# A transformer block on one Trainium2 core: the first half of the values taken from x before it is normalised, the second half moved up behind it

## The chip, the cores and the metric

The kernel runs on one core of a Trainium2 chip. The core has five engines with an instruction stream each: TensorE (matmuls; PE in the profile, its weight loads PEld), VectorE (DVE), ScalarE (ACT), GpSimd (POOL) and SyncE (SP, which only issues DMAs). The metric is the device time of one execution in microseconds; a profiled execution has its own time, and a span from its first to its last instruction.

## The reference, cut to what is computed

One layer, one batch row, 1024 tokens, width 1024, 16 heads of 64, all in fp32:

```python
mod = c_act @ ada_w[l] + ada_b[l]            # c_act = silu(c)
sh1, sc1, g1, sh2, sc2, g2 = [m[:, None, :] for m in jnp.split(mod, 6, axis=-1)]
h = rmsnorm(x, ln1_g[l]) * (1.0 + sc1) + sh1
p = h @ w_in[l]
q, k, v, cb, cc, cx, ga, gb = jnp.split(p, split_at, axis=-1)
q = rmsnorm(q.reshape(b, s_len, SB_HEADS, SB_HEAD_DIM), q_norm_g[l])
k = rmsnorm(k.reshape(b, s_len, SB_HEADS, SB_HEAD_DIM), k_norm_g[l])
y_a = stick_breaking_attention(q, k, v)
y_b = cb * causal_dwconv(cc * cx, conv_w[l])
merged = (jax.nn.sigmoid(ga) * (y_a @ w_branch_a[l])
          + jax.nn.sigmoid(gb) * (y_b @ w_branch_b[l]))
x = x + g1 * (merged @ w_out[l])
h = rmsnorm(x, ln2_g[l]) * (1.0 + sc2) + sh2
f = (jax.nn.silu(h @ w_ffn_gate[l]) * (h @ w_ffn_up[l])) @ w_ffn_down[l]
x = x + g2 * f
```

The attention has no softmax. For a block of 128 queries and the keys up to it, the weight of key s is sigmoid(z_ts) times the product of 1 - sigmoid(z_tj) over the keys j between s and t. The kernel gets that product from a scan along the keys, and multiplies the scanned values with the differences of neighbouring rows of v, plus the last row of v of each block.

The value projection is linear, which the change uses: with a = ln1_g (1 + sc1), row t of v is (1/rms_t) times (x_t a) @ W, plus sh1 @ W, and the last term is one row, the same for every token.

## The kernel before, in words

Every fp32 product is made of three fp32r matmuls. An operand is split into a high part (ScalarE, an activation that rounds) and a low part (VectorE, operand minus high part); the product is high x high, high x low, low x high, summed in one PSUM bank. PSUM has eight banks of 128 x 512. Each matmul goes over 128 rows of the contraction, so a product over the width of 1024 has 8 steps of three matmuls.

The stages, with their places in the profile (us from the start of the span):

- **Opening, 0 to 72.** x is loaded twice: by tokens (`xq`), for the mean square of each token, and transposed (`xts`, by channels). L184 loads `cab`, the row c broadcast to 128 partitions. Silu(c) is made of it with a Sigmoid and a product. For each tile of 128 channels, `mod_sum` (L246 to L254) makes two dot products of 1024 columns on VectorE (L250), one for the scale and one for the shift; `norm_x` (L287) multiplies the tile with a and 1/rms, where `bcast` (L277 to L279) has spread 1/rms over the partitions with fp32 matmuls; `make_hi` (L292, ScalarE) and `make_lo` (L296, VectorE) add the shift and split. `mm_tok` (L299 to L309) multiplies 128 tokens with the weights. In the opening it takes the first 512 columns of the values: 8 token tiles x 8 channel tiles x 3 matmuls, all eight PSUM banks open at once. Eight fp32 matmuls over raw tokens (L262) stand ahead. `finish_v` (L417 to L423) copies the result and stores it to `d_v[0]`. The loads come in order on SyncE's queue.
- **Key projection, 72 to 134.** `mm_tok` again, two times 8 tiles of 512 columns. `finish_k` normalises them by heads and turns them. Beside it, the generator `factors()`, driven by `more()`, builds on VectorE the sums of tiles of x that later products use (`xts`, `ts`, `dsh` of L137 and L371) and writes them to DRAM.
- **Gates, queries and the convolution's inputs, to 566**, by products of sums of blocks (L132 to L134, combined on VectorE at L137).
- **Attention, 566 to about 997.** Per head and block i of 128 queries: `att_scores` (L808, L809: z, then a Sigmoid on ScalarE at L810), `att_scan` (L818, VectorE, length 128 (i + 1)), `att_trans` (L832 transposes on TensorE, L835 high part on ScalarE, L836 low part on VectorE) and, for every second block, `att_av` (L847, L848). The transposes of block i - 2 and the products of block i - 3 come with the scores of block i (`attention`, L863 on). `att_dv` makes the differences of the value rows (vb minus va, L137) and splits them; `load_v` and `load_vlast` read the values back.
- **Fillers.** Between the steps of attention, TensorE takes other matmuls from the generator `fillers()` (L912 on): first the second half of the values (L927 to L929, 256 columns at a time, two groups of 256, 16 tiles), then the gated convolution (16 tiles, L908 to L910 with evacuation L137), then the projection of branch B (16 tiles, L908 to L910), whose evacuation multiplies with the sigmoid of gate B (L982, VectorE) and goes to `d_mb`. The first 16 yields of it (HEAD) come ahead of the heads. What is left then is spread by a count: each step of attention yields a number (F_Z per bank of scores, F_T per transposed block), each filler step yields 1.3 or 0.65, and `fill` (L994) keeps the two sums in the proportion `ratio`. So these numbers, and not the time that things take, set the order on TensorE.
- **Branch A, 997 to 1100.** Its projection, times the sigmoid of gate A, plus `mb` of branch B. Then the output projection, the second norm and the FFN to the end.

The order on TensorE, and that of attention's instructions on VectorE, is the order of the program text and of the counts above.

Of the kernel before, what the change touches and what calls it, by code (L numbers as in the profile page):

```python
# [9 lines left out]
F32 = mybir.dt.float32  # L10
# [20 lines left out]
def block_kernel(tc, x, x_t, cols, ada_1, ada_2, ada_row, w_q, w_kv, w_v1, w_cg, w_a, w_b, w_o, w_g, w_u, w_d, out):  # L31
# [38 lines left out]
    d_v = [drp.tile([n, P + 1, KT, P], F32, name=f"d_v{n}_{e}") for e, n in enumerate((4, 2, 2))]  # L70
# [5 lines left out]
    d_mb = drp.tile([KT, P, T], F32, name="d_mb")  # L76
    d_g = [drp.tile([P, D], F32, name=f"d_g{e}") for e in range(2)]
# [15 lines left out]
    nc.scalar.activation(one, one, AF.Sigmoid)  # L93
# [75 lines left out]
    sa_ = ExitStack()  # L169
    adp = sa_.enter_context(tc.tile_pool(name="adp", bufs=1, side="right", reuse_waits="tile"))  # L170
# [9 lines left out]
    xqs = [bigp.tile([P, 4, D], F32, tag="big", bufs=4, name=nm("xq")) for n in range(2)]  # L180
    xq = [xqs[i // 4][:, i % 4, :] for i in range(8)]
    rs = sp.tile([P, T], F32, name="rs")
    cab = sp.tile([P, D], F32, name="cab")
    nc.scalar.dma_start(cab, ada_row[0:1, :].broadcast_to([P, D]))  # L184
    hh = [big() for n in range(2)]
    junk = [h_[:, :2, :].rearrange("p a t -> p (a t)") for h_ in hh]

    def load_xq(i0_, i1_):
        for i in range(i0_, i1_):
            nc.sync.dma_start(xq[i], x[i * P:(i + 1) * P, :])  # L190
# [3 lines left out]

    wq = []
    MC0, MC = 3, 2
    ads = []

    def load_ada(e):
        ad = adp.tile([P, 2, D], F32, tag="ada", bufs=2, name=nm("ada")) if e % 3 < 2 else sp.tile(  # L200
            [P, 2, D], F32, tag="ada", bufs=1, name=nm("ada"))
        nc.sync.dma_start(ad, ada_1[e])
        ads.append(ad)
# [26 lines left out]

    load_xq(0, 4)
    load_ada(0)
    load_xq(4, 8)
    load_x(0)
    load_wq(0)
    load_ada(1)
    load_x(1)
    load_ada(2)
    load_x(2)
    load_wq(1)  # L240
    load_x(3)
# [4 lines left out]
    def mod_sum(e):  # L246

        msum = sp.tile([P, 2], F32, tag="msum", bufs=2, name=nm("msum"))
        for m in range(2):
            nc.vector.tensor_tensor_reduce(out=ads[e][:, m], in0=ads[e][:, m], in1=cab, scale=1.0, scalar=0.0, op0=ALU.mult,  # L250
                                           op1=ALU.add, accum_out=msum[:, m:m + 1])
        nc.vector.scalar_tensor_tensor(out=a1[:, e:e + 1], in0=msum[:, 1:2], scalar=acp[:, e:e + 1],
                                       in1=ln1[:, e:e + 1], op0=ALU.add, op1=ALU.mult)
        nc.scalar.activation(mod[:, 0, e:e + 1], msum[:, 0:1], AF.Identity, bias=acol[:, 0, e:e + 1])  # L254


    ss1 = sp.tile([P, 8], F32, name="ss1")
    rsp = [ps_tr() for n in range(2)]
    warm = ps_pj()
    rts = []  # L260
    for i in range(8):
        nc.tensor.matmul(warm, ident, xq[i][:, :512], start=True, stop=True)  # L262
        if i % 2:
            nc.vector.tensor_tensor_reduce(out=junk[1], in0=xq[i], in1=xq[i], scale=1.0, scalar=0.0, op0=ALU.mult,
                                           op1=ALU.add, accum_out=ss1[:, i:i + 1])
        else:
            nc.scalar.activation(junk[0], xq[i], AF.Square, accum_out=ss1[:, i:i + 1])
        if i == 1:
            nc.scalar.activation(rs, cab, AF.Sigmoid)
            nc.vector.tensor_tensor(out=cab, in0=cab, in1=rs, op=ALU.mult)  # L270
        if i % 4 == 3:
            rts.append(rstd_of(ss1[:, i - 3:i + 1], 1.0 / D, sp, 4, eng=nc.vector))
        if i == 3:
            mod_sum(0)
            load_ada(3)
# [60 lines left out]
    for k in range(KT - 1):  # L336
# [11 lines left out]
        if k % 2 == 0:  # L348
            load_wq(k // 2 + 2)
# [1279 lines left out]
```

## Time and profile before

| | |
|---|---|
| time, median of 3 executions | 1825.74 us (1823.97 to 1827.85) |
| the profiled execution | 1827.39 us, its span 1825.6 us |
| TensorE's granted clock, mean of the span | 0.997 |
| VectorE busy | 1356.8 us, 74% of the span, 1957 instructions |
| ScalarE busy | 794.9 us, 44%, 1494 instructions |
| GpSimd busy | 368.5 us, 20%, 277 instructions |
| HBM read, written | 245.22 MB, 110.66 MB |

Read it like this. Busy time is summed per engine over the whole span; TensorE's share is quoted with the prediction. A row of the groups has the line, the engine, the operation, what it writes and reads, the tile, a count, the busy time with the mean of one instruction in ns, and the idle time of that engine just ahead with what ended most of it. A row of a timeline has the start, the duration (of one, or with x8 of a run of eight records), the engine, the line and the operation, and in brackets the wait ahead of it with its releaser. A row of the windows has the stretch A:B, its length, the busy time with the count of instructions for TensorE, its weight loads, VectorE, ScalarE and GpSimd, then the mean granted clock, the share of the DMA engines and GB/s. A row of the waits has who waited for what, with the sum in us, the count and the longest. An fp32 matmul is two records in the profile, an fp32r one is one.

### The profile page before, as it was taken

The page shows a single profiled execution, that of the slowest core. Times are in us where ns is not written, and L with a number is a line of the kernel's source. Part 1 is how long each engine was busy: PE and PEld are TensorE (multiplying, and loading weights), DVE is VectorE, ACT ScalarE, POOL GpSimd, SP SyncE. Part 2 cuts the span into 40 slices and gives each one's busy share as a digit, 9 for nine tenths or more (in the row PEclk, how much of TensorE's full clock was granted, in tenths as well). Part 3 has the DMA queues.
Part 4 walks back from the last instruction along what each step waited for, and adds up shares of the span by engine and source line. Part 5 has one row for each costly group of instructions (what it writes and reads, how often), then busy time and mean ns, then how long its engine had stood idle before and what let it go on. Part 6 is the DMA issues. An engine that isn't in the chain of part 4 may idle for free.

```text
span 1825.6 us, 24915 instructions
## 1 busy us (share of the span) xinstructions
PE 1799.5 (99%) x8829; PEld 1502.2 (82%) x8829; DVE 1356.8 (74%) x1957; ACT 794.9 (44%) x1494; POOL 368.5 (20%) x277
## 2 busy tenths in 40 slices
PE   7999999999999999999999999999999999999999
PEld 5788778887879988888888788877888888878887
DVE  7873877779872899999887554689977888644776
ACT  3452653333343666666665221663444344322321
POOL 0043328323230000000000000115534544200000
PEclk9999999999999999999999999999999999999999
DMA  9687551227748566689654546324533344299766
GB/s 394 199 319 292 181 184 69 87 84 252 273 152 247 149 180 190 196 222 304 163 141 151 174 162 217 124 88 161 196 149 140 148 166 159 104 363 325 279 230 220
DMA packets 163508, 357.50 MB, mean 196 GB/s; under 512 B 15464, under 2 KB 60848, under 8 KB 161208
## 3 DMA queue, kind: packets, MB, share of 16 engines
q1 hardware_dynamic: 130920, 289.65, 47.5%
q10 hardware_dynamic: 31456, 62.59, 9.5%
q0 software_dynamic: 1008, 3.67, 0.5%
q8 instruction: 71, 1.16, 0.3%
q14 instruction: 53, 0.43, 0.1%
HBM read 245.22 MB, written 110.66 MB: 195 GB/s over the span
## 4 chain that ended last, share of the span: by engine, by line
PE 86%; DVE 7%; DMA 4%; issue 1%; ACT 1%; POOL 0%; SPq 0%; ACTq 0%; DVEq 0%; POOLq 0%
PE e L133 7%; PE e L132 7%; PE e L134 7%; PE pj L134 5%; PE pj L132 5%; PE pj L133 5%; PE pj L309 5%; PE pj L908 5%; PE pj L910 4%; PE pj L909 4%; PE e L1456 4%; PE e L1458 4%; PE e L1457 4%; PE tr L832 3%; PE o L848 2%; PE z L808 2%
## 5 line engine op out<-in xcount | busy, mean ns | idle before, releaser
L818 DVE TENSOR_TENSOR_SCAN pt<-pt,mk 128x128 f32<-128x128 f32 (+7 forms) x128 | 172.4, 1347 | 13.0 <-ACT pt L810 13.0
L132 PE MATMUL e<-big,whi 128*128 128x512 f32 x352 | 137.9, 392 | 2.0 <-DVE c L137 2.0
L133 PE MATMUL e<-big,whi 128*128 128x512 f32 x352 | 137.7, 391 | 0.0
L134 PE MATMUL e<-big,wlo 128*128 128x512 f32 x352 | 137.5, 391 | 0.0
L123 POOL TENSOR_SCALAR rs_m<-ss 128x1 f32<-128x1 f32 x8 | 2.3, 282 | 642.9 <-ACT xn L1259 642.9
L137 DVE TENSOR_TENSOR c<-e,c 128x512 f32<-128x512 f32 x138 | 92.8, 686 | 51.4 <-PE e L134 50.5
L132 PE MATMUL pj<-big,whi 128*128 128x512 f32 x320 | 125.2, 391 | 1.4 <-DVE c L137 1.4
L134 PE MATMUL pj<-big,wlo 128*128 128x512 f32 x320 | 124.8, 390 | 0.0
L133 PE MATMUL pj<-big,whi 128*128 128x512 f32 x320 | 124.6, 389 | 0.0
L1456 PE MATMUL e<-whi,f 128*128 128x512 f32 (+1 forms) x319 | 121.8, 382 | 1.1 <-DMA f<-d_f 1.1
L137 DVE TENSOR_TENSOR c<-pj,c 128x512 f32<-128x512 f32 x140 | 93.0, 681 | 38.9 <-PE pj L134 38.4
L1457 PE MATMUL e<-wlo,f 128*128 128x512 f32 (+1 forms) x319 | 121.8, 382 | 0.0
L1458 PE MATMUL e<-whi,f 128*128 128x512 f32 (+1 forms) x319 | 121.6, 382 | 0.0
L836 DVE TENSOR_TENSOR atl<-tr,ath 128x512 fp32r<-128x512 f32 (+1 forms) x192 | 103.9, 550 | 19.4 <-ACT ath L835 17.9
L810 ACT ACTIVATE pt<-z,rq 128x512 f32<-128x512 f32 (+1 forms) x192 | 104.7, 575 | 26.6 <-PE z L809 26.4
L908 PE MATMUL pj<-big,whi 128*128 128x512 f32 x256 | 114.0, 445 | 0.0
L309 PE MATMUL pj<-whi,big 128*128 128x512 f32 x352 | 109.3, 396 | 3.9 <-ACT big L292 3.9
L137 POOL TENSOR_TENSOR ws<-raw,raw 128x512 f32<-128x512 f32 x40 | 56.3, 1407 | 275.5 <-DMA raw<-w_cg 165.8
L137 DVE TENSOR_TENSOR wlo<-raw,whi 128x512 fp32r<-128x512 f32 x116 | 88.3, 766 | 31.6 <-ACT whi L463 31.0
L463 ACT ACTIVATE whi<-raw 128x512 fp32r<-128x512 f32 x116 | 72.4, 628 | 86.9 <-PE pj L133 45.4
L835 ACT ACTIVATE ath<-tr 128x512 fp32r<-128x512 f32 (+1 forms) x192 | 93.3, 487 | 30.0 <-PE tr L832 29.1
L133 PE MATMUL e<-rl,whi 128*128 128x512 f32 x264 | 102.8, 389 | 1.5 <-DVE rl L137 1.5
(258 smaller groups left out, 4998.6 us busy)
## 6 DMA issues: line engine op xcount, KB each, us to landing
f<-d_f SPq DMA_DIRECT2D x77, 512.0 KB, 4.3
d_f<-fs SPq DMA_DIRECT2D x70, 512.0 KB, 3.2
raw<-w_cg SPq DMA_DIRECT2D x40, 512.0 KB, 3.8
raw<-w_u SPq DMA_DIRECT2D x26, 512.0 KB, 3.2
raw<-w_g SPq DMA_DIRECT2D x25, 512.0 KB, 3.4
ad<-ada ACTq DMA_DIRECT2D x19, 512.0 KB, 4.5
ada<-ada SPq DMA_DIRECT2D x8, 1024.0 KB, 11.6
d_t<-ts SPq DMA_DIRECT2D x16, 512.0 KB, 3.7
```

The source lines that it names most:

```text
L132: nc.tensor.matmul(ps, wh[:, k, :], fh[:, k, :], start=(k == 0), stop=False)
L133: nc.tensor.matmul(ps, wh[:, k, :], fl[:, k, :], start=False, stop=False)
L134: nc.tensor.matmul(ps, wl[:, k, :], fh[:, k, :], start=False, stop=(k == 3))
L137: eng.tensor_tensor(out=out, in0=a, in1=b, op=op)
L309: nc.tensor.matmul(ps, a, b, start=(k == 0 and q == 0), stop=(k == KT - 1 and q == 2))
L810: nc.scalar.activation(pt[:, off + s0:off + s0 + m], z[:, :m], AF.Sigmoid, scale=rq[:, 1, i, h:h + 1])
L818: nc.vector.tensor_tensor_scan(out=pt[:, rev], data0=pt[:, rev], data1=mk[:, rev], initial=1.0, op0=ALU.mult, op1=ALU.max)
L836: nc.vector.tensor_tensor(out=tl[:, :nb, c0:c0 + P], in0=src, in1=th[:, :nb, c0:c0 + P].bitcast(F32), op=ALU.subtract)
L908: nc.tensor.matmul(ps, wh, rh_, start=(k == 0), stop=False)
L1456: nc.tensor.matmul(o, sh, w[0][:, c], start=(j == 0), stop=False)
L1457: nc.tensor.matmul(o, sh, w[1][:, c], start=False, stop=False)
L1458: nc.tensor.matmul(o, sl, w[0][:, c], start=False, stop=(j == NJ - 1))
```

## The change

- **The opening's first half.** The first 512 columns of the values are now made from x times a, not normalised: `raw_hi` and `raw_lo` split x a1, `real` multiplies. So a step needs the scale's dot product only (`scale_sum`); the shift's comes later (`shift_sum`). The tokens' mean squares (`square`, all on ScalarE) are needed only when a result is evacuated: `finish_raw` multiplies its rows by 1/rms. Six token tiles run through all channels; the two others (`tail`) run behind, around `bcast`.
- **The shift's part** of those columns, the row sh1 @ W, is made in the key projection: `shift_row` adds up eight products of weights and shifts on VectorE into `zb`, and `put_row` sums its partitions with two small matmuls and stores the row (`d_b`) and its negative (the row that stands ahead of the first token). `turn_vlast` adds it to the last rows.
- **Silu(c)** is spread by two one-row fp32 matmuls with an activation Silu behind each, from `crow`, a load of one row in place of the broadcast one. Four fp32 matmuls on a constant (`NW = 4`) stand where the eight on tokens stood. The activation that the program starts with (its table with it) is Silu in place of Sigmoid.
- **The second half of the values** (512 columns) comes right behind, from normalised x, in the form that the opening had. The values' fillers are gone, and with them the input `w_v1`; `w_kv` has one block more.
- **Loads** of the opening: tokens and modulation share a ring of five tiles of 512 KB (`load_ring`), the modulation's two parts are loaded one by one, the tokens after the channels.
- **Gate B.** Branch B's result is copied by ScalarE to `d_mb`; the product with gate B is made in branch A on GpSimd, with the gate loaded there.
- **The counts.** F_S adds 0.05 (i + 1) or so to a block's yield, FILL is 2.0 x 16 x 5.2 in place of 2.5, HEAD counts 16 yields of 0.65. The gated convolution takes its tiles in pairs of channels.

The diff, cut:

```diff
-d_v = [... for e, n in enumerate((4, 2, 2))]
+d_v = [... for e, n in enumerate((4, 4))]
-nc.scalar.activation(one, one, AF.Sigmoid)
+nc.scalar.activation(one, one, AF.Silu)
-nc.scalar.dma_start(cab, ada_row[0:1, :].broadcast_to([P, D]))
+crow = sp.tile([1, D], F32, name="crow")
+nc.scalar.dma_start(crow, ada_row[0:1, :])
...
+def raw_hi(k):
+    for n in range(2):
+        nc.scalar.activation(hh[n][:, k, :], xt(k, n), AF.Copy, scale=a1[:, k:k + 1])
+def raw_lo(k):
+    for n in range(2):
+        nc.vector.scalar_tensor_tensor(out=hl[n][:, k, :], in0=xt(k, n), scalar=a1[:, k:k + 1],
+                                       in1=hh[n][:, k, :].bitcast(F32), op0=ALU.mult, op1=ALU.subtract)
...
+for e in range(2):
+    t = ps_pj()
+    nc.tensor.matmul(t, mk[0:1, D - P:], crow[:, e * 512:e * 512 + 512], start=True, stop=True)
+    nc.scalar.activation(cab[:, e * 512:e * 512 + 512], t, AF.Silu)
+for e in range(NW):
+    nc.tensor.matmul(warm, ident, mk[:, 512:], start=True, stop=True)
...
+for k in range(KT):
+    real(psr, k, range(MC), wq)
+    if k + 1 < KT:
+        raw_hi(k + 1)
+        split_lo(k + 1)
+    if k + 2 < KT:
+        scale_sum(k + 2)
+        split_hi(k + 2)
+    if k + 1 < KT:
+        raw_lo(k + 1)
+    real(psr, k, range(MC, NR), wq)
...
+tail(0, KB)
+for i in range(NR):
+    finish_raw(i)
...
+bcast(0)
+bcast(1)
+tail(KB, KT)
...
+            if cc == 1 and 0 < i < 6:
+                if i < 5:
+                    shift_row(i - 1)
+                else:
+                    put_row()
...
-    F_Z, F_T, F_O = 0.2,0.3,0
+    F_Z, F_T, F_S = 0.2, 0.3, 0.05
-        yield F_Z
+        yield F_Z + F_S * ((i - 1) % 8 + 1)
...
-            nc.vector.tensor_tensor(out=mb, in0=ps, in1=sb, op=ALU.mult)
+            nc.scalar.activation(mb, ps, AF.Copy)
-    FILL = 2.5 * 16 * 5.2
+    FILL = 2.0 * 16 * 5.2
-    FILL -= 1.3 * HEAD
+    FILL -= 0.65 * HEAD
...
+        sb = fp.tile([P, 512], F32, tag="yr", bufs=2, name=nm("sgb"))
+        nc.sync.dma_start(sb, d_sgb[m, :, n * 512:(n + 1) * 512])
+        nc.gpsimd.tensor_tensor(out=mb, in0=mb, in1=sb, op=ALU.mult)
```

How the order on the engines moves is shown at three places. The first is TensorE at the start of the program. Before (big is x's parts, whi and wlo the weights', dm the identity):

```order
L262 MATMUL pj_182<-xq_143,dm 128x512 x4
L262 MATMUL pj_182<-xq_144,dm 128x512 x4
L279 MATMUL tr_180<-dm,rs_r_194 128x128 x4
L279 MATMUL tr_181<-dm,rs_r_213 128x128 x4
L309 MATMUL pj_247<-whi_163,big_148 128x512
```

And now, in the lines of the changed program (mk is the constant mask):

```order
L326 MATMUL pj_173<-crow,mk 128x512
L326 MATMUL pj_176<-crow,mk 128x512
L329 MATMUL tr_172<-mk,dm 128x512 x4
L294 MATMUL pj_196<-whi_157,big_144 128x512
L294 MATMUL pj_197<-whi_157,big_144 128x512
L294 MATMUL pj_196<-wlo_158,big_144 128x512
```

The tokens' matmuls and the spread of 1/rms no longer stand ahead of the projection; the two one-row matmuls and the four on a constant do.

The second place is TensorE at the start of attention (z is a bank of scores, sqt, skh and skl are queries and keys). Before, around the first score:

```order
L808 MATMUL z_5117<-skh_4864,sqt_4863 128x128
L927 MATMUL pj_4979<-whi_4892,big_148 128x256
L928 MATMUL pj_4979<-wlo_4893,big_148 128x256
L929 MATMUL pj_4979<-whi_4892,big_217 128x256
L927 MATMUL pj_4979<-whi_4892,big_148 128x256
L928 MATMUL pj_4979<-wlo_4893,big_148 128x256
L809 MATMUL z_5117<-skl_4865,sqt_4863 128x128
L929 MATMUL pj_4979<-whi_4892,big_217 128x256
L927 MATMUL pj_5006<-whi_4878,big_149 128x256
```

And now:

```order
L900 MATMUL z_5313<-skh_5232,sqt_5231 128x128
L901 MATMUL z_5313<-skl_5233,sqt_5231 128x128
L1000 MATMUL pj_5319<-big_145,whi_5200 128x512
L1001 MATMUL pj_5319<-big_147,whi_5200 128x512
L1002 MATMUL pj_5319<-big_145,wlo_5201 128x512
L900 MATMUL z_5325<-skh_5232,sqt_5231 128x256
L901 MATMUL z_5325<-skl_5233,sqt_5231 128x256
L900 MATMUL z_5333<-skh_5232,sqt_5231 128x384
L901 MATMUL z_5333<-skl_5233,sqt_5231 128x384
...
L924 MATMUL tr_5342<-dm,pt_5193 128x128
```

The tiles of values that followed the first score are gone; the scores of the next blocks follow it with one group of three filler matmuls between, and the transpose of the first block (L924) has one more group ahead of it.

The third place is VectorE where the key projection begins (vs is a stored value tile, wlo a low part of weights, xts and dsh belong to `factors()`). Before:

```order
L420 COPY vs_582<-pj_252 128x512
L420 COPY vs_594<-tr_254 128x512
L137 TENSOR_TENSOR dsh<-mod 128x4
L63 TENSOR_TENSOR wlo_1007<-raw_1004,whi_1006 128x1024
L371 SCALAR_TENSOR_TENSOR xts<-xts,dsh 128x512 x4
L137 TENSOR_TENSOR xts<-xts 128x512 x2
```

And now:

```order
L477 COPY vs_879<-pj_576 128x512
L540 TENSOR_SCALAR zb_915<-raw_954,mod 128x512
L542 SCALAR_TENSOR_TENSOR zb_915<-raw_954,mod,zb_915 128x512
L228 TENSOR_TENSOR wlo_891<-raw_888,whi_890 128x1024
L477 COPY vs_897<-pj_578 128x512
L477 COPY vs_909<-tr_580 128x512
L138 TENSOR_TENSOR dsh<-mod 128x4
L428 SCALAR_TENSOR_TENSOR xts<-xts,dsh 128x512 x3
L542 SCALAR_TENSOR_TENSOR zb_915<-raw_995,mod,zb_915 128x512
L428 SCALAR_TENSOR_TENSOR xts<-xts,dsh 128x512
```

The eight products of the shift's row stand among the last value tiles and the sums of `factors()`; two of them come ahead of the last two copies of value tiles.

More of the change, by code (lines that the diff above doesn't have):

```diff
@@ L309, in mm_tok, with real, store_v, finish_raw @@
                     nc.tensor.matmul(ps, a, b, start=(k == 0 and q == 0), stop=(k == KT - 1 and q == 2))
+    def real(pss, k, ts, w):
+        for parts in ((0,), (1,), (2,)):
+            for i in ts:
+                mm_tok(pss[i], i, w, k, k + 1, parts)
+    def store_v(vs, h, i):
+        nc.scalar.dma_start(d_v[h][:, 1:, i].rearrange("r p d -> p r d"), vs.rearrange("p (r d) -> p r d", d=P))
+    def finish_raw(i):
+        vs = gw.tile([P, 512], F32, tag=("whi", "wlo")[i % 2], bufs=GS, name=nm("vs"))
+        r = rts[i // 4][:, i % 4:i % 4 + 1]
+        if i % 2:
+            nc.vector.tensor_scalar(out=vs, in0=psr[i], scalar1=r, scalar2=None, op0=ALU.mult)
+        else:
+            nc.scalar.activation(vs, psr[i], AF.Copy, scale=r)
+        store_v(vs, 0, i)
@@ L752, in load_v @@
         pr = h // 2
[L753 removed]
+        d = d_v[h // 8][pr % 4]
         t_ = ("vb", "va")[e]
```

283 lines of the change are left out of this document (144 added, 139 removed).

## The prediction

> **What bounds the kernel now.** The page first, then what TensorE waited for, then its timeline.
>
> ```profile
> PE 1799.5 (99%) x8829; PEld 1502.2 (82%) x8829; DVE 1356.8 (74%) x1957; ACT 794.9 (44%) x1494; POOL 368.5 (20%) x277
> PE   7999999999999999999999999999999999999999
> ```
> ```profile
> PE pj L262 <- DMA xq<-x: 7.4, 3, 4.5
> PE pj L309 <- ACT big L292: 3.9, 8, 1.0
> ```
> TensorE is busy in all of the 40 slices but the first. So a change is worth what it takes off TensorE's list, plus what it takes off the idle time of the opening, less the new idle time that it makes. The two longest waits are both in the opening. TensorE's timeline there:
>
> ```profile
> 4.55 2.05 PE L262 MATMUL pj<-xq,dm 128*128 128x512 f32 x2 [4.55 <-DMA xq<-x]
> 13.90 5.36 PE L262 MATMUL pj<-xq,dm 128*128 128x512 f32 x8 [2.25 <-DMA xq<-x]
> 19.10 1.05 PE L279 MATMUL tr<-dm,rs_r 128*128 128x128 f32 x8
> 20.35 1.16 PE L279 MATMUL tr<-dm,rs_r 128*128 128x128 f32 x8 [0.19 <-POOL rs_r L124]
> 21.80 0.98 PE L309 MATMUL pj<-whi,big 128*128 128x512 f32 x3 [0.29 <-ACT big L292]
> 35.13 0.73 PE L309 MATMUL pj<-whi,big 128*128 128x512 f32 x2 [0.39 <-ACT big L292]
> 41.25 0.74 PE L309 MATMUL pj<-whi,big 128*128 128x512 f32 x2 [0.39 <-ACT big L292]
> 71.99 0.39 PE L309 MATMUL pj<-whi,big 128*128 128x512 f32 x1
> ```
> Everything ahead of 21.80 us is no work of the projection: L262 keeps the clock up, L279 spreads 1/rms. The first half of the values (192 matmuls of 512 columns) then runs from 21.80 to 71.99, in steps of 41.25 - 35.13 = 6.12 us. The cost of such a matmul when nothing is waited for, from a dense stretch (21 rows, first and last):
>
> ```profile
> 559.65 0.39 PE L132 MATMUL pj<-ft,whi 128*128 128x512 f32 x1
> 564.18 0.39 PE L134 MATMUL pj<-big,wlo 128*128 128x512 f32 x1
> ```
> 4.53 us / 20 = 0.2265 us, so a step's 24 matmuls need 5.44 us, not 6.12. The chain of waits shows who sets the 6.12:
>
> ```profile
> 35.11 1.41 DVE big L296 x2
> 36.52 1.14 DVE ada L250
> 37.66 1.14 DVE ada L250
> 38.84 0.23 DVE a L252
> 39.10 1.30 DVE xts L287
> 40.48 0.73 ACT big L292
> ```
> VectorE's two dot products of the modulation, the normalisation and the low parts, with the first high part between, are the chain. So the opening holds 72.0 - 192 x 0.2265 = 28.5 us in which TensorE does no projection.
>
> **The change part by part.**
>
> 1. *Start of the raw half.* Its first matmul needs crow, two one-row fp32 matmuls, two Silu, one dot product, two high parts of x, one high part of the weights.
>
> ```profile
> 1.27 0.35 ACTq L184 DMA_DIRECT2D cab<-ada_row  x1
> 4.64 0.15 DVE L109 TENSOR_SCALAR cst<-cst 128x1 f32<-128x1 f32 x1 [3.51 <-DMA cst<-cols]
> 407.65 0.58 ACT L686 ACTIVATE c<-pj 128x512 f32<-128x512 f32 x1
> ```
> ```profile
> 0.00:20.00 20.00, 12.57 (x24) 5.08 (x24) 9.47 (x23) 7.43 (x13) 3.60 (x10) 0.91 0.92 360
> ```
> crow (4 KB) takes the place of cab on ScalarE's queue, issued at 1.27 us; I let it land as cst does, at about 4.7. An fp32 matmul of 512 columns is two records, 2.05 us in the first row above, 1.34 in the x8 row with its waits; two at the first price end at 8.8. Then Silu 0.58, the dot product 1.14 with its 0.23, two high parts at 0.73, one of the weights at 0.6 (estimate from the 0.58 row): 12.6, and with six hand-overs of about 0.1, **13.3 us**. At 360 GB/s the first three loads (1.6 MB) have come by 9, so they don't decide.
>
> 2. *Raw half, six tiles.* 18 matmuls a step, 4.08 us; VectorE's step falls to one dot product 1.37, low parts 1.41 and weights 0.68: 3.5 us, below TensorE's. 8 x 4.08 = 32.6, plus 0.4 for the first step, whose low parts come late: 46.3. The statistics of the rows (eight squares) are off the path: loads of 16 MB at some 0.4 MB/us end at about 43, and the two tiles kept back (48 matmuls, 10.9 us, part of them ahead of the spread of 1/rms) cover the rest. If that cover is gone the price is about 1 us. The spread costs 2.2 us as now (L279). 46.3 + 10.9 + 2.2 = 59.4.
>
> 3. *Second half behind it.* 192 x 0.2265 = 43.5; VectorE's step is one dot product 1.37, 1.30, 1.41, 0.68 = 4.8 under 5.44, so TensorE sets it. With 0.6 for changing banks: end at **103.5 us** against 72.0. Term: **+31.5**.
>
> 4. *What leaves attention.*
>
> ```profile
> 566.55 0.28 PE L927 MATMUL pj<-whi,big 128*128 128x256 f32 x1
> 572.30 0.28 PE L927 MATMUL pj<-whi,big 128*128 128x256 f32 x1
> ```
> ```profile
> L927 PE MATMUL pj<-whi,big 128*128 128x256 f32 x128 | 37.3, 292 | 0.0
> L982 DVE TENSOR_TENSOR mb<-pj,sgi 128x512 f32<-128x512 f32 x16 | 10.9, 681 | 1.7 <-PE pj L910 1.5
> ```
> 48 matmuls lie between those starts: 0.1198 us each; three lines of 128 are 384: **-46.0** of TensorE's time. From VectorE go the gating products (16 x 0.68) and eight splits, some 16 us.
>
> 5. *The new start of attention.* Filler tiles stood between the first score and the next ones, and now the heads begin at once (second order piece).
>
> ```profile
> 578.88 0.42 DVE L818 TENSOR_TENSOR_SCAN pt<-pt,mk 128x128 f32<-128x128 f32 x1 [12.99 <-ACT pt L810]
> 580.11 0.69 DVE L137 TENSOR_TENSOR vb<-vb,va 128x512 f32<-128x512 f32 x1 [0.80 <-DMA vb<-d_v]
> 592.87 0.68 DVE L818 TENSOR_TENSOR_SCAN pt<-pt,mk 128x256 f32<-128x256 f32 x1
> ```
> 14 us lay between first and second scan and cost nothing, since TensorE had tiles of values. Now the second scan is queued on VectorE behind the difference vb, which waits for its load (landing at 580.1, and one weight load more ahead of it). TensorE reaches the transpose of block 1 some 2 us too early, and that of block 7 another 2. Bounds 0 and 14; I take **+4**, near what the loads and scans give.
>
> 6. *The pace of the heads.*
>
> ```profile
> 665.14 0.41 DVE L818 TENSOR_TENSOR_SCAN pt<-pt,mk 128x128 f32<-128x128 f32 x1
> 863.37 0.41 DVE L818 TENSOR_TENSOR_SCAN pt<-pt,mk 128x128 f32<-128x128 f32 x1
> ```
> ```profile
> 640.00:865.00 225.00, 225.00 (x1373) 196.76 (x1372) 204.65 (x290) 147.20 (x332) 0.00 (x0) 1.00 0.76 217
> 865.00:965.00 100.00, 100.00 (x607) 87.34 (x607) 88.88 (x125) 64.68 (x147) 0.00 (x0) 1.00 0.58 155
> ```
> Eight heads take 198.2 us, 24.8 each, all TensorE's. The new filler per head is 14 groups of three matmuls where 17 stood (counted in the order): 9 x 0.2265 + 0.2 = 2.2 less, so 22.6. VectorE is busy 204.65/225 x 24.8 = 22.5 us a head with about six filler operations; now about five while the gated convolution is the filler: 21.8, and 2.3 us of its head are idle, in small waits for ScalarE. If all that idle time can be squeezed, nothing is lost; if it all stays, a head takes 24.1 and eight lose 12 us. The fill now follows the scan lengths (F_S), so I take that 1.3 of 2.3 stay: 23.1, **+4** over eight heads. In the heads of branch B VectorE has lost the product: (88.88/100 x 24.9) - 1.2 = 20.9, and TensorE sets the pace.
>
> 7. *VectorE in the key projection.*
>
> ```profile
> 72.00:120.00 48.00, 48.00 (x224) 39.70 (x223) 38.88 (x58) 23.08 (x35) 16.85 (x14) 1.00 0.86 301
> 82.25 2.73 DVE L371 SCALAR_TENSOR_TENSOR xts<-xts,dsh 128x512 f32<-128x512 f32 x4
> ```
> Eight products at 0.68 and a split are 6.1 us more on VectorE, ahead of the first key tile's normalisation (third order piece). It has 9.1 us idle there, and six banks let TensorE run 32 us ahead, so I take **+0.6**, of bounds 0 and 6.1. The two small fp32r matmuls are 0.45 of it.
>
> 8. *At nothing:* the 16 products with gate B on GpSimd in branch A (GpSimd is idle there, each tile has 5.4 us of matmuls as cover, and only the addition waits, not a PSUM bank; without cover 16 x 1.4 = 22 us); the evacuation by ScalarE (147 of 225 us busy); the changed first table (ScalarE has idle time at both places); the four weight loads and the stores.
>
> Sum: 31.5 - 46.0 + 4 + 4 + 0.6 = **-5.9 us**. The profiled execution took 1827.39 (span 1825.6), so 1821.5; it stands 1.65 above the median shown, so **1819.8**.
>
> The Trainium skill, "TensorE: Matmul & The Clock Gate", section "What's actually happening", says that TensorE starts at half rate and gets its full clock only after about 3.4 us of sustained work. This trace agrees: 2.05 us for the first pair against 0.45 a record later, and a mean clock of 0.91 in the first 20 us. The page doesn't say whether a one-row matmul counts as work; if it doesn't, the rule speaks for the late start below.
>
> **Rivals.**
>
> *Attention stays TensorE's.* If the first heads and the pace cost 0.5 us together, -13.4: **1812.3**. For it: no stall of TensorE between 640 and 965 although VectorE is at 91%. Against: 97% is asked of it now.
>
> *VectorE takes over attention* (the slow side). Its 2.3 us of idle time a head stay: 12 us over eight heads, (20.9 + 2.3 - 22.6) x 7 = 4 in the rest, the start 4: 20 in place of 8, **1831.8**. It loses from 0.8 us of kept idle time on, and is slower than before from about 17.6 us in all. For it: scan, low parts and products run in one order with TensorE waiting for each scan. Against: the idle time came while TensorE was the pace.
>
> *The opening starts late, or the keys stall.* If the four warming matmuls run at 2.05 us behind the one-row ones, the first real matmul comes at 8.8 + 8.2 = 17, 3.7 later; if the 6.1 us of item 7 aren't hidden, 5.5 more than I took. Either gives **1823.5 to 1825.3**. This is also the case in which the change does less than it says.
>
> **How the numbers follow.** Forecast 0.50 (1816 to 1824), attention all TensorE's 0.20, VectorE takes over 0.14, late start or keys 0.16. A measurement of this kernel tells about 0.2%, 3.7 us, from no change: faster is below 1822.1, slower above 1829.4. Faster: 0.38 of the forecast's 0.50 plus 0.20 = 0.58. Same: 0.12 + 0.14 + 0.02 = 0.28. Slower: 0.12 + 0.02 = 0.14. Range: down to the all-TensorE case and up to where the slow side begins, 1811.5 to 1829.5.
>
> **What would show it.** In the new profile: the first projection matmul at 13 us and steps of 4.1 then 5.4 us; the key projection starting at 103 or 104; about 4 us of waits for scans or loads in the first head; heads of 23 us, then 22.6; VectorE near 95% in the first eight. It would be wrong if a head takes 24 us or more, if TensorE's waits for VectorE in attention pass 15 us, or if the opening ends past 108.

## The result, and the profile after

| | before | after |
|---|---|---|
| median of 12 executions | 1825.23 us | 1830.57 us |
| ratio to before, with its 95% interval | | 1.0029 (1.0016 to 1.0042) |
| the profiled execution, its span | 1827.39, 1825.6 us | 1830.19, 1828.4 us |
| start of the program to the first filler matmul of attention | 566.11 us | 597.19 us (+31.1) |
| from there to the first matmul of the output projection | 524.66 us | 496.83 us (-27.8) |
| from there to the end | 734.83 us | 734.38 us (-0.4) |

The change is 5.3 us slower by the medians, against a forecast of 5.9 us faster. The two profiled executions stand 2.8 us apart, because that of before lies 2.2 us above its median and that of after 0.4 below; stages are compared between these two. One of the 12 executions of the changed kernel ran at 3478.30 us, with a mean granted clock of 0.899; it is left out of the ratio. The bounds of the stages are these rows of TensorE's timeline, first of before (the first is the first tile of values, the second the output projection):

```profile
566.11 0.36 PE L927 MATMUL pj<-whi,big 128*128 128x256 f32 x1
...
1090.77 0.39 PE L1236 MATMUL e<-whi,big 128*128 128x512 f32 x1
```

and of after, where the first filler is the gated convolution:

```profile
597.19 0.48 PE L1000 MATMUL pj<-big,whi 128*128 128x512 f32 x1
...
1094.02 0.39 PE L1300 MATMUL e<-whi,big 128*128 128x512 f32 x1
```

All that comes ahead of attention costs 31.1 us more, close to what was forecast (31.5, and 0.6 for the keys). The middle stretch gives back 27.8 us, where 38 were expected (46.0 less the 4 and 4 of the start and the pace). So the loss is to be looked for there. What TensorE waited for in the changed kernel:

```profile
PE pj L1000 <- DVE sgi L1147: 7.3, 3, 6.3
PE pj L326 <- DMA crow<-ada_row: 5.5, 1, 5.5
PE tr L924 <- DVE pt L910: 3.8, 6, 1.4
...
PE z L900 <- DMA skh<-d_k: 1.6, 1, 1.6
...
PE z L901 <- DMA skl<-d_k: 1.0, 1, 1.0
```

The second row stands ahead of all work. The third to fifth are the start of attention and the heads. The longest wait is new (in the kernel before, TensorE has no wait for the product with gate A) and lies in branch A: TensorE waits for a PSUM bank until VectorE (L1147) has multiplied an earlier result with gate A. Its longest piece:

```profile
1087.11 0.80 PE L1000 MATMUL pj<-ya,whi 128*128 128x512 f32 x1 [6.32 <-DVE sgi L1147]
```

VectorE itself is late, and that builds up over many tiles. Its row of branch A, then GpSimd's product with gate B (L1144), then SyncE's issues (L1143 loads gate B into sgb, L1141 branch B's result into mb, L1139 gate A into sgi, L508 weights):

```profile
1036.51 0.69 DVE L1147 TENSOR_TENSOR sgi<-pj,sgi 128x512 f32<-128x512 f32 x1 [1.94 <-DMA sgi<-d_sga]
...
1044.85 0.69 DVE L1147 TENSOR_TENSOR sgi<-pj,sgi 128x512 f32<-128x512 f32 x1 [4.86 <-DMA sgi<-d_sga]
...
1050.10 0.69 DVE L1147 TENSOR_TENSOR sgi<-pj,sgi 128x512 f32<-128x512 f32 x1 [1.97 <-DMA sgi<-d_sga]
...
1056.99 0.69 DVE L1147 TENSOR_TENSOR sgi<-pj,sgi 128x512 f32<-128x512 f32 x1 [3.41 <-DMA sgi<-d_sga]
```

```profile
1044.27 1.29 POOL L1144 TENSOR_TENSOR mb<-mb,sgb 128x512 f32<-128x512 f32 x1 [7.07 <-issue]
1049.53 1.29 POOL L1144 TENSOR_TENSOR mb<-mb,sgb 128x512 f32<-128x512 f32 x1 [3.97 <-DMA mb<-d_mb]
```

```profile
1045.59 0.32 SPq L1143 DMA_DIRECT2D sgb<-d_sgb  x1
1045.96 0.42 SPq L1141 DMA_DIRECT2D mb<-d_mb  x1
1046.48 0.38 SPq L1139 DMA_DIRECT2D sgi<-d_sga  x1
1050.85 0.32 SPq L1143 DMA_DIRECT2D sgb<-d_sgb  x1
1051.23 0.42 SPq L508 DMA_DIRECT2D raw<-w_a  x1
1051.74 0.38 SPq L1141 DMA_DIRECT2D mb<-d_mb  x1
1052.22 0.38 SPq L1139 DMA_DIRECT2D sgi<-d_sga  x1
```

Read the three together. Counted from 0, these are gate B of tile 10, branch B's result of tile 9 and gate A of tile 8, and then the same for tiles 11, 10 and 9 with a load of weights between. The product (of tile 8) ends at 1044.27 + 1.29 = 1045.56, and at 1045.59 SyncE issues a load of gate B: it had waited for that product, since gate B has two buffers. Only behind it come the loads of mb and of gate A. Gate A lands at about 1050.1, 3.6 us later, and VectorE starts at that moment; mb lands at 1049.5, and GpSimd starts its next product at that moment. Then the circle begins again. So each tile takes a product and a load's latency one after the other. From 1036.51 to 1074.24 there are six such rounds, 6.3 us each in the mean, and TensorE needs 24 x 0.2265 = 5.44 for a tile.

The rounds are not alike. From product to product, 1044.27 to 1049.53 are 5.26 us, a little under what TensorE needs; 1049.53 to 1056.39 are 6.86, and there the weight load L508 (512 KB) stands in front of the load of mb. So most of the excess comes in the rounds in which weights stand in the chain. In gate_only, a run shown below, it is the same: 5.1 to 5.3 us without a weight load, 6.4 to 6.8 with one. One round of the changed kernel is long without any (1066.65 to 1073.69); why is not shown.

The waits for gate A make VectorE late, but only 1.0 of the 7.3 us of TensorE's wait stands right behind them. The longest piece, 6.3 us, goes by another load that stands in the same place, the first weights of the output projection (w_o, L1107; ScalarE makes their high part in L1111, VectorE their low part in L1112):

```profile
1073.69 1.28 POOL L1144 TENSOR_TENSOR mb<-mb,sgb 128x512 f32<-128x512 f32 x1 [5.75 <-DMA mb<-d_mb]
1075.00 0.32 SPq L1143 DMA_DIRECT2D sgb<-d_sgb  x1
1075.41 0.38 SPq L1107 DMA_DIRECT2D raw<-w_o  x1
1079.26 1.15 ACT L1111 ACTIVATE whi<-raw 128x512 fp32r<-128x512 f32 x2 [8.11 <-DMA raw<-w_o]
1079.92 2.36 DVE L1112 TENSOR_TENSOR wlo<-raw,whi 128x512 fp32r<-128x512 f32 x2 [4.99 <-ACT whi L1111]
1086.37 0.68 DVE L1147 TENSOR_TENSOR sgi<-pj,sgi 128x512 f32<-128x512 f32 x1
```

The product ends at 1074.97, then SyncE issues gate B and right behind it the weights; ScalarE waits for them, VectorE for ScalarE, and VectorE's next product with gate A, which frees the bank, comes behind that in VectorE's order. After the idle time TensorE also runs slower for a while: its granted clock was 0.50 from 1087.10 to 1090.00.

```profile
1087.10:1090.00 2.90, 2.90 (x7) 2.32 (x8) 1.78 (x3) 0.63 (x1) 0.48 (x1) 0.50 0.01 3
1090.00:1094.00 4.00, 4.00 (x19) 3.29 (x18) 1.59 (x3) 0.63 (x1) 0.00 (x0) 1.00 0.76 277
```

### The profile page after: what moved, and what is told of

Its sections match the earlier page's. It is cut to its first block, busy times and chain, and to the rows that moved or that the text cites. A ratio compares the mean times of both kernels' runs of the same rounds, so it can differ in the third digit from the quotient of the medians.

```text
span 1828.4 us, 24603 instructions
## 1 busy us (share of the span) xinstructions
PE 1795.6 (98%) x8635; PEld 1490.9 (82%) x8635; DVE 1360.4 (74%) x1964; ACT 815.2 (45%) x1527; POOL 388.9 (21%) x293
## 5 line engine op out<-in xcount | busy, mean ns | idle before, releaser
L294 PE MATMUL pj<-whi,big 128*128 128x512 f32 x448 | 132.9, 393 | 0.0
L1144 POOL TENSOR_TENSOR mb<-mb,sgb 128x512 f32<-128x512 f32 x16 | 21.6, 1353 | 494.3 <-DMA mb<-d_mb 454.5
L928 DVE TENSOR_TENSOR atl<-tr,ath 128x512 fp32r<-128x512 f32 (+1 forms) x192 | 103.3, 550 | 14.9 <-ACT ath L927 12.8
L133 PE MATMUL e<-rh,whi 128*128 128x512 f32 x264 | 102.7, 389 | 0.0
L135 PE MATMUL e<-rh,wlo 128*128 128x512 f32 x264 | 102.7, 389 | 0.0
```

What stands on the lines that cost most here:

```text
L133: nc.tensor.matmul(ps, wh[:, k, :], fh[:, k, :], start=(k == 0), stop=False)
L135: nc.tensor.matmul(ps, wl[:, k, :], fh[:, k, :], start=False, stop=(k == 3))
L294: nc.tensor.matmul(ps, a, b, start=(k == 0 and q == 0), stop=(k == KT - 1 and q == 2))
L928: nc.vector.tensor_tensor(out=tl[:, :nb, c0:c0 + P], in0=src, in1=th[:, :nb, c0:c0 + P].bitcast(F32), op=ALU.subtract)
```

## The experiments

Ratios are to the kernel before, on the same chip, with their 95% intervals; runs on different chips are compared by these ratios. Theory Q (the order on SyncE's queue) stood against G (GpSimd's product is too slow), E (the loss lies elsewhere), and later K (the kind of queue) and B (the shared buffers).

### The product with gate B

**Undone in the changed kernel** (gate_back): the loads of gate B and the product on VectorE return to branch B.

```diff
-            nc.scalar.activation(mb, ps, AF.Copy)
+            nc.vector.tensor_tensor(out=mb, in0=ps, in1=sb, op=ALU.mult)
...
-        nc.gpsimd.tensor_tensor(out=mb, in0=mb, in1=sb, op=ALU.mult)
```

> The changed kernel with one part undone: the product with gate B is back in branch B (VectorE, at the evacuation). Theory Q (queue): in branch A the load of the gate (sgb) waits on SyncE's queue for one of two buffers, that is for GpSimd's product of two tiles before, and the loads of mb and of gate A queued behind it come late, so VectorE and then TensorE's bank wait. Then TensorE's waits for sgi in branch A (7.3 us in the profile of the change) fall to 0 to 2.5 and the time falls by 5 to 8 us: ratio to before 0.998 to 1.001. Rival G (GpSimd's product itself, 1.3 to 2.5 us, is too slow) expects the same here. Rival E (the loss lies in the opening, at the start of attention and in the pace of the heads; a stall in branch A would only move) expects 1.002 to 1.004 as the change has.

Measured: 1822.39 us, ratio 0.9989 (0.9980 to 0.9998); no wait for sgi. So the rest of the change makes the kernel about 2 us faster, and the move of gate B loses all of that and more. Rival E falls.

**Done alone in the kernel before** (gate_only), the same edit the other way round.

> The kernel before with this one part of the change alone: ScalarE copies branch B's result, gate B is loaded and multiplied in branch A on GpSimd. Theories Q and G: waits of TensorE for sgi of 5 to 9 us appear in branch A, 4 to 8 us slower than before, ratio 1.002 to 1.0045. Rival E: less work for VectorE in the last heads and no loss behind, ratio 0.999 to 1.001.

Measured: 1831.12 us, ratio 1.0041 (1.0027 to 1.0055). The stall comes with the edit (in this kernel L1079 is the product with gate A; the profiled execution took 1827.40 us, 3.7 less than the median):

```profile
PE pj L908 <- DVE sgi L1079: 4.6, 1, 4.6
```

0.9989 and 1.0041 together give 1.0030, the change itself 1.0029: the parts add up.

**One load on another queue** (sgb_queue; run again as sgb_queue2):

```diff
-        nc.sync.dma_start(sb, d_sgb[m, :, n * 512:(n + 1) * 512])
+        nc.gpsimd.dma_start(sb, d_sgb[m, :, n * 512:(n + 1) * 512])
```

> The changed kernel, with one load moved: the gate's tile (sgb) is loaded from GpSimd's queue in place of SyncE's; the product stays on GpSimd. Theory Q: nothing stands behind that load any more, TensorE's waits for sgi fall from 7.3 to under 2.5 us, the time by 5 to 7 us, ratio 0.998 to 1.001. Rival G (GpSimd too slow): waits of 6 to 8 us stay, ratio 1.002 to 1.004. Rival E: no change either, 1.002 to 1.004.

> The kernel of sgb_queue once more, as the base of the two runs beside it on the same chip. If the gain of the queue is real: ratio to before 0.996 to 0.9985 and no wait of TensorE for sgi over 1 us; if the first figure was chance, 0.999 to 1.001.

Measured: 1819.47 us, ratio 0.9971 (0.9959 to 0.9982), and 1821.05, 0.9977 (0.9968 to 0.9987). All waits of TensorE from 985 to 1090 us, and VectorE's rows there:

```profile
PE pj L1000 <- ACT mb L1042: 0.6, 1, 0.6
```

```profile
1044.15 0.69 DVE L1147 TENSOR_TENSOR sgi<-pj,sgi 128x512 f32<-128x512 f32 x1 [2.10 <-PE pj L1002]
1049.59 0.69 DVE L1147 TENSOR_TENSOR sgi<-pj,sgi 128x512 f32<-128x512 f32 x1 [1.47 <-PE pj L1002]
```

Rounds of 5.44 us, and now VectorE waits for TensorE (L1002). GpSimd's product is the same 1.29 us, so G falls. The load of w_o that was late in the change is issued 85.0 us after the last scan begins (1062.78), in the change 94.8 us after it (1075.41). The middle stretch takes 485.63 us here (596.40 to 1082.03), 39.0 less than before; in sgb_queue2 it is 487.45, 37.2 less.

**The product on VectorE** (gate_dve), the loads as in the change:

```diff
-        nc.gpsimd.tensor_tensor(out=mb, in0=mb, in1=sb, op=ALU.mult)
+        nc.vector.tensor_tensor(out=mb, in0=mb, in1=sb, op=ALU.mult)
```

> The changed kernel with the product mb x sgb of branch A on VectorE in place of GpSimd; all loads stay on SyncE's queue in the same two buffers. Theory Q: the loads are released by a VectorE instruction instead, the queue is the same, so TensorE's waits for sgi stay at 4 to 9 us, ratio 1.002 to 1.004. Rival G: 0.7 us on VectorE in place of 1.3 to 2.5 on GpSimd, waits under 2.5, ratio 0.998 to 1.001. Rival E: 1.002 to 1.004.

Measured: 1826.01 us, ratio 1.0007 (0.9998 to 1.0016), between Q's figures and G's:

```profile
PE pj L1000 <- DVE sgi L1147: 3.6, 5, 1.1
```

The product is one link of the circle; at 0.69 in place of 1.29 us, the circle is shorter and half of the stall is left. This run alone would not have decided.

**The order on SyncE's queue alone** (sgb_after): gate B of a tile is loaded behind gate A of the same tile. Queue, buffers and engines stay.

```diff
+        with tc.issue_after(ld_a.ins):
             nc.sync.dma_start(sb, d_sgb[m, :, n * 512:(n + 1) * 512])
```

> The changed kernel with one load later on the same queue: on SyncE's queue the load of gate B of a tile stands behind the load of gate A of the same tile, in place of two tiles ahead of it. Buffers, engines and queue are those of the change. Theory Q: nothing that is needed stands behind a load that waits for the product any more, TensorE's waits for sgi fall from 7.3 to under 2 us, ratio 0.997 to 0.999. Rival K (it was the kind of queue, the loads land later on SyncE's): waits of 5 to 8 us stay, 1.002 to 1.004. Rival G (GpSimd's product too slow): the same, 1.002 to 1.004.

Measured: 1820.84 us, ratio 0.9974 (0.9965 to 0.9983); no wait for sgi (L1148 is the product with gate A here):

```profile
1043.82 0.69 DVE L1148 TENSOR_TENSOR sgi<-pj,sgi 128x512 f32<-128x512 f32 x1 [1.17 <-PE pj L1002]
1049.26 0.69 DVE L1148 TENSOR_TENSOR sgi<-pj,sgi 128x512 f32<-128x512 f32 x1 [2.16 <-PE pj L1002]
```

This is the direct test, and Q stands: the same loads on the same queue in another order are worth 0.55% of the time, about 10 us. K falls.

**Buffers of its own for gate B** (sgb_wx2), two as before, the steady order as in the change:

```diff
-        sb = fp.tile([P, 512], F32, tag="yr", bufs=2, name=nm("sgb"))
+        sb = wx.tile([P, 512], F32, tag="sgb", bufs=2, name=nm("sgb"))
```

> The changed kernel with two buffers of its own for gate B, in place of the two that it shares with the tiles of the attention output; queue and order of the steady state as in the change. Theory Q: in the steady state nothing changes, waits for sgi of 4 to 8 us, ratio 1.0015 to 1.004. Rival B (the shared buffers make the first loads late, and that is never caught up): waits under 2 us, 0.997 to 0.9995.

Measured: 1832.20 us, ratio 1.0036 (1.0024 to 1.0049). B falls:

```profile
PE pj L1000 <- DVE sgi L1147: 7.4, 4, 6.4
```

**The mended move alone in the kernel before** (gate_only_q): gate_only, with the gate's load on GpSimd's queue.

> The kernel before with gate B moved to branch A on GpSimd, and the gate's load on GpSimd's queue. If the parts of the change add up (gate_back 0.9989 without the move, the mended change 0.9974 with it): 0.998 to 1.0, no wait for sgi over 1 us. If the move costs in the kernel before for another reason than the queue: 1.001 to 1.004.

Measured: 1823.39 us, ratio 0.9994 (0.9985 to 1.0002); no wait for sgi. By itself the mended move gains about 1 us, which the interval doesn't tell from nothing; in the changed kernel, where it is compared with gate_back, some 3 us (0.9974 against 0.9989, intervals that touch).

### The other terms of the sum

All of these start from sgb_queue. The base ran beside dve_less, keys_q and both on one chip (sgb_queue2); for the others, whose chip it did not run on, its ratio is taken as 0.9974, the mean of its two.

**More work for VectorE in the first eight heads** (dve_more): one copy in place at each evacuation of the gated convolution.

```diff
             nc.vector.tensor_tensor(out=y, in0=ps, in1=y, op=ALU.mult)
+            nc.vector.tensor_copy(out=y, in_=y)
```

> The changed kernel with the gate's load on GpSimd's queue (1819.5 us, ratio 0.9971), plus one more VectorE operation (a copy of 512 columns in place, 0.35 to 0.7 us) at each of the 16 evacuations of the gated convolution: 6 to 11 us more for VectorE in the first eight heads. Theory P (TensorE sets the pace of the heads, VectorE has room left): 0 to 3 us slower than that kernel, ratio 0.9965 to 0.999, TensorE's waits for scans in the heads rise by under 3 us. Rival V (VectorE is at its limit in the first eight heads, my slow rival): 6 to 11 us slower, ratio 1.0005 to 1.0035.

Measured: 1824.96 us, ratio 1.0001 (0.9992 to 1.0009). The copy took 0.42 us:

```profile
699.92 0.42 DVE L1018 COPY cy<-cy 128x512 f32<-128x512 f32 x1
```

16 of them are 6.7 us, and the time rose by about 0.27%, 4.9 us. That lies between P's figures, which end at 0.999, and V's, which begin at 1.0005. So most of what VectorE gets there is paid for, though TensorE's listed waits for VectorE in attention rise by 2.1 us only (4.4 for scans and 1.8 for low parts, against 3.7 and 0.4).

**Less work for VectorE** (dve_less): the convolution's low parts on GpSimd.

```diff
-            nc.vector.tensor_tensor(out=yl, in0=y, in1=yh.bitcast(F32), op=ALU.subtract)
+            nc.gpsimd.tensor_tensor(out=yl, in0=y, in1=yh.bitcast(F32), op=ALU.subtract)
```

> That base with the 16 low parts of the gated convolution (0.67 us each on VectorE, 10.8 us, in the first eight heads) made on GpSimd, which is idle there. Theory V2 (in the first eight heads VectorE is within a few per cent of being the limit, as 5.5 us for 6.6 us of extra copies said): the heads get shorter by 1 to 5 us in all. Rival P (TensorE's own work sets 22.9 us a head; added work shows, removed work doesn't): under 1 us. Rival C (GpSimd slows VectorE beside it): 2 to 8 us slower.

Measured: 1822.94 us, ratio 0.9984 (0.9975 to 0.9993), beside 0.9977 of the base on the same chip. No gain. The operation takes 1.77 us on GpSimd, and TensorE waits longer for scans (6.5 us, 3.8 in the base):

```profile
L1021 POOL TENSOR_TENSOR ybl<-cy,ybh 128x512 fp32r<-128x512 f32 x16 | 28.3, 1770 | 204.6 <-ACT ybh L1020 204.6
```

V2's gain didn't come, and the trace shows where most of it went. From 636 to 820 us the 13 low parts that VectorE no longer makes are 8.8 us of its work in the base. But three of its other groups got slower beside GpSimd, by 6.5 us in all: the scans of 1024 (2514 in place of 2281 ns) and of 256 (849, 680), and the low parts of the value differences, here and then in the base:

```profile
L138 DVE TENSOR_TENSOR vt<-vb,vt 128x512 fp32r<-128x512 f32 x8 | 8.6, 1078 | 0.0
...
L138 DVE TENSOR_TENSOR vt<-vb,vt 128x512 fp32r<-128x512 f32 x8 | 5.4, 672 | 0.0
```

So VectorE was spared little, as rival C has it, though its 2 to 8 us of loss are not told from nothing. Whether a VectorE with less to do would make the heads shorter stays open.

**The fill without the scan's weight** (fs0):

```diff
-    F_Z, F_T, F_S = 0.2, 0.3, 0.05
+    F_Z, F_T, F_S = 0.2, 0.3, 0.0
```

> The same base (ratio 0.9971) with F_S = 0: the fill no longer gets more weight at the long scans. It tests the step of the forecast that put 4 us on the pace of the heads because the fill follows the scans. Theory P: TensorE waits more often before a transpose of a long block, by 1 to 4 us in all, ratio 0.997 to 0.9995. Rival V: without it VectorE sets the pace, waits of 8 to 15 us, ratio 1.001 to 1.005. If the count doesn't matter: within 1 us, 0.9965 to 0.9977.

Measured: 1824.02 us, ratio 0.9990 (0.9980 to 1.0000): some 3 us slower than the base, P's size and not V's. P's way isn't shown: TensorE's waits for scans are 3.2 us, 3.7 in the base, and those for low parts 2.0 against 0.4. From the first filler to the last scan it took 383.5 us, as the base did (381.4 and 383.2); the longer stretch is the one behind it, from the last scan to the output projection, 106.9 us against 104.2.

**More filler ahead of the heads** (head22):

```diff
-    HEAD, TAIL = 16, 10.0
+    HEAD, TAIL = 22, 10.0
```

> The same base with 22 in place of 16 yields of filler ahead of the heads: 18 matmuls, 4.1 us. Theory S (the start of attention costs what its stalls show: 1.3 and 0.8 us for the loads of the keys, 2 to 2.5 for the first scans): the waits for the keys go, those for the scans stay or shrink, 1.5 to 4 us faster, ratio 0.995 to 0.9963. Rival (the filler is only taken from later places, where TensorE then waits): 0.9963 to 0.998.

Measured: 1825.05 us, ratio 1.0003 (0.9994 to 1.0011), worse than both said. The waits for keys are gone, but a third filler tile now needs a PSUM bank, and its evacuation needs a tile `cy` from DRAM:

```profile
PE pj L1000 <- DVE cy L1017: 8.0, 1, 8.0
```

```profile
612.19 2.78 SPq L1022 DMA_DIRECT2D d_yb<-ybh  x1
...
615.50 2.23 SPq L1011 DMA_DIRECT2D cy<-d_y  x3
```

The load of cy (L1011) stands on SyncE's queue behind the loads of two heads and two stores. The base issues it at about the same time (614.75); here it is needed earlier. So what stands on a queue decides again, but there is no circle of product and latency as in branch A.

**Two warming matmuls in place of four** (nw2):

```diff
-    NLD, MC, NW, KB = 5, 2, 4, 2
+    NLD, MC, NW, KB = 5, 2, 2, 2
```

> The same base with two in place of four fp32 matmuls that warm TensorE. In the profile of the change these end at 15.1 us, while the first operands are there at 13.3. Theory W (they delay the first product): it starts at 13.0 to 13.6 and the second half of the values, the keys and all behind come 1 to 1.8 us earlier, ratio 0.9960 to 0.9967 as far as that can be told. Rival C (the clock is not up yet): it starts earlier, but its first matmuls take over 0.45 us a piece, and the six-tile steps catch up; under 0.5 us, ratio 0.9967 to 0.9975.

Measured: 1820.97 us, ratio 0.9982 (0.9972 to 0.9991). The first product starts where the operands are there:

```profile
13.26 1.22 PE L294 MATMUL pj<-whi,big 128*128 128x512 f32 x2 [0.39 <-ACT whi L217]
```

That is W's start, but the base itself is not steady there: its first product starts at 15.15 in one profile and at 13.79 in the other. The last matmul of the keys comes at 196.4 us, against 198.0 and 196.7, and the first filler of attention at 595.35, against 596.40 and 595.41. The first scores wait longer for their keys (2.8 us, against 1.3 and 1.6). So the gain is 0.3 to 1.6 us at the keys and 0.1 to 1.1 at the first filler, and in the total nothing of it can be told.

**The first keys on GpSimd's queue** (keys_q):

```diff
+        q = nc.sync if h else nc.gpsimd
...
-            nc.sync.dma_start(sqt[es].bitcast(F32), d_q[e][pr, e0:e0 + DH, :])
+            q.dma_start(sqt[es].bitcast(F32), d_q[e][pr, e0:e0 + DH, :])
```

> That base with the six loads of the first head's queries and keys on GpSimd's queue. On SyncE's they stand behind a weight load that waits 7.7 us for its buffer. Theory S: the waits of TensorE for keys at the start (1.3 and 0.8 us) go, that for the first scan shrinks, 1 to 4 us faster than the base. Rival (the memory that the loads go to, or the values' load behind, is late anyway): waits of the same size under another name, within 1 us.

Measured: 1828.66 us, ratio 1.0020 (1.0011 to 1.0029), slower than both theories have it. GpSimd issues two of the six loads early, and then none for 6.5 us:

```profile
593.82 0.75 POOL L832 DMA_DIRECT2D sqt<-d_q  x1 [21.36 <-PE pj L135]
594.57 0.73 POOL L833 DMA_DIRECT2D skh<-d_k  x1
601.78 0.69 POOL L834 DMA_DIRECT2D skl<-d_k  x1 [6.48 <-issue]
```

The scores then wait 4.3 and 1.7 us. What holds the third load isn't shown by the profile. Nor is all of the loss there: behind the output projection this run takes 737.2 us, the base 733.8, and why is open.

**All three together** (both): nw2, dve_less and keys_q.

> The base with all three: low parts on GpSimd, the first keys on GpSimd's queue, two warming matmuls. If each does what its theory says: 4 to 8 us faster than the base, about 1812 to 1816. If the rivals hold: within 2 us of the base.

Measured: 1827.95 us, ratio 1.0018 (1.0009 to 1.0026). It follows keys_q.

## Why the prediction was wrong, step by step

**Item 8 failed.** It put the product on GpSimd at nothing, because "only the addition waits, not a PSUM bank", with 5.4 us of matmuls as cover. The engine times in that were right (1.29 us a product). What it left out is that the moved step adds a load to SyncE's queue, ahead of the loads that the evacuation of earlier tiles needs and ahead of weights, and that this load waits for the product. The evacuation itself then comes late, and with it the bank. The runs give about 10 us (1.0029 against 0.9974 with the order alone changed) where the forecast had 0. The upper bound that it named, 22 us without cover, came from the engine's time and had nothing to do with it. The prediction had not followed that queue, though the moved step issues a DMA of its own.

Of the 10 us, the waits show 7.3. From the last scan to the output projection, branch A takes 113.5 us in the change and 104.2 in sgb_queue. Of the other 2 us, 1.4 are the slower clock behind the stall: the six steps from the matmul at 1087.11 to that at 1089.83 take 2.72 us, where 6 x 0.2265 is 1.36. The waits don't list this.

**The rest of the sum held.** With the order mended, 1819.5 to 1821.1 us were measured; the forecast was 1819.8. By the ratios that is 4.2 to 5.3 us faster than before, where 5.9 were forecast. That it comes so near is in part luck: the first filler of attention alone starts at 596.40 and 595.41 us in the base's two profiles and at 599.26 in sgb_after, whose program is the same up to there.

- *The opening.* The steps of 4.08 us came as forecast:

```profile
12.74 2.90 PE L329 MATMUL tr<-mk,dm 128*128 128x512 f32 x4
15.08 1.02 PE L294 MATMUL pj<-whi,big 128*128 128x512 f32 x2
...
16.39 1.52 PE L294 MATMUL pj<-whi,big 128*128 128x512 f32 x6
...
20.47 1.52 PE L294 MATMUL pj<-whi,big 128*128 128x512 f32 x6
```

  The first product starts at 15.08, not at 13.3: the four warming matmuls (L329) end there, and item 1 counted what is ahead of the operands on the other engines, but not these on TensorE's own list. In this profile they are the late-start rival at half its price; in other runs with the same four the first product starts anywhere from 13.33 (dve_less) to 15.15 (sgb_queue), and hardly any of it reaches the total (nw2). (Item 1's parts add up to 12.8 and not 12.6, which changes nothing.) The last matmul of the keys comes at 197.93 us, 32.7 after that of the kernel before, for which 32.1 were forecast; in the kernel before it stands at 165.21, so the key projection ended there and not at 134. The mean clock of 0.91 in the first 20 us, which the prediction took as a sign of the start at half rate, isn't one: the views show 0.50 only later, from 13.90 to 16.00 us, and 1.00 from 4.50 to 6.60, where the first pair took its 2.05.
- *The start of attention*, forecast at +4: TensorE's waits there are 2.4 us for scans and 2.6 for the first keys. The size was right; that half of it would be a load of keys was not seen.
- *The pace of the heads*, forecast at 23.1 us. Two scans nine heads apart, and the stretch of most of the first eight heads:

```profile
661.11 0.41 DVE L910 TENSOR_TENSOR_SCAN pt<-pt,mk 128x128 f32<-128x128 f32 x1
...
867.77 0.41 DVE L910 TENSOR_TENSOR_SCAN pt<-pt,mk 128x128 f32<-128x128 f32 x1
```

```profile
636.00:820.00 184.00, 183.21 (x1139) 159.32 (x1138) 176.63 (x249) 128.81 (x292) 0.00 (x0) 1.00 0.79 229
```

  206.66 / 9 = 22.96 us a head, and VectorE is busy for 176.63 of 184 us, 96%. dve_more shows that it has little room left, so the slow rival had its mechanism right; it only stayed below its price. "Attention all TensorE's" (22.6 us) didn't come. It didn't come in the later heads either, for which the forecast had 22.6 too: from the scan at 867.77 to that at 936.87, three heads, a head takes 23.0.

**The slow side came by a way that no rival had.** All three looked at engines that take turns (VectorE in attention, TensorE's start, VectorE at the keys). None of them was a queue of DMAs.

## What to carry to other kernels

When a step is moved to an idle engine, write down the DMAs that it brings, the buffer that each of them waits for, and what stands behind it on its queue. A load that waits for the consumer of an earlier tile makes every load behind it part of one chain: product, latency, product. Count the weights among them: here the longest stall went by a load of weights for the next stage. A load for a later tile belongs behind the loads that the present tile needs, or on another queue, and a look at the queue's order shows it before anything runs.

## What the runs showed that was not expected

- The Trainium skill, "DMA: Bandwidth & Descriptors", section "Issuing engines are not separate DMA queues", says that starting DMAs on several engines only saves the time that the sequencer takes to start them, usually small. Here one load of 256 KB a tile, moved from SyncE's queue to GpSimd's, was worth about 10 us (1.0029 against 0.9971 and 0.9977), and the same load put later on SyncE's queue was worth as much. The gain was not bandwidth or the time to issue (0.32 us), but the wait at the head of the queue. The measurement decides: a queue's waits have to be counted with it. And the other queue is no cure by itself, as keys_q shows.
- VectorE and GpSimd can slow each other where they overlap (dve_less: 1.77 us on GpSimd for an operation of 0.67 on VectorE, and VectorE's own groups slower beside it). In the changed kernel, GpSimd makes products from 1011.22 to 1013.76 and from 1015.33 to 1016.85, and these VectorE rows, 0.69 us elsewhere, stand beside them:

```profile
1012.54 1.77 DVE L1148 TENSOR_TENSOR sgi<-sgi,mb 128x512 f32<-128x512 f32 x1 [1.44 <-POOL mb L1144]
...
1015.61 1.78 DVE L138 TENSOR_TENSOR wlo<-raw,whi 128x512 fp32r<-128x512 f32 x1
```

- VectorE at 96% showed in the total before it showed in TensorE's waits: 6.7 us more work cost about 4.9 us (dve_more), while TensorE's listed waits for it in attention rose by 2.1.
